# Retention stage of a hybrid decoder block: the norm goes to POOL and ScalarE, gate weights are split earlier, gate banks are single, and ten modulation rows move in

## The chip, the cores and the metric

The kernel runs on one core of a Trainium2 chip. The metric is the device time of one execution in microseconds. Three runs of the kernel before took 2174.5, 2175.4 and 2175.61 us; the median is 2175.4 us.

An engine has a queue of its own and works through it strictly in order, and engines meet through semaphores. The engines are named as in the profile: PE is TensorE (PEld its weight loads), DVE is VectorE, ACT is ScalarE, POOL is GpSimd, SP is SyncE, which here only issues transfers. PSUM has eight banks of 128 x 512 float32 numbers; matmuls write there. SBUF is the memory that all engines read.

## What is computed

A decoder block on 1024 tokens with 1024 channels: a conditioning vector gives six rows of shifts and scales (`w_ada`), a mixer runs retention and dilated attention side by side, and an MLP follows. The part that the change touches is retention: 4 heads, key width 256, value width 512, in 8 chunks of 128 tokens, then a norm over each head's 512 channels, a gain and offset, and a gate:

```
mod = jax.nn.silu(c) @ w_ada[l] + b_ada[l]
...
s = jnp.einsum('bhid,bhjd->bhij', qi, ki) * inner_decay[None]
o = (jnp.einsum('bhij,bhje->bhie', s, vi)
     + jnp.einsum('bhid,bhde->bhie', qi, state) * q_decay[None, :, :, None])
state = (state * chunk_decay[None, :, None, None]
         + jnp.einsum('bhjd,bhje->bhde', ki * k_decay[None, :, :, None], vi))
...
ro = ((ro - mu) * lax.rsqrt(var + GN_EPS)).transpose(0, 2, 1, 3).reshape(B, S, RET_V_W)
ro = (ro * gn_g.astype(jnp.float32) + gn_b.astype(jnp.float32)).astype(h.dtype)
ret_out = (jax.nn.silu(rg) * ro) @ w_ret_out
```

## The kernel before

Every float32 product is made of three matmuls: each operand is split into a high part (a rounded copy, usually by ScalarE) and a low part (the operand less its high part, usually by DVE), and low x high, high x low and high x high are summed in PSUM (`mm3`; lines 207, 209 and 211 are its three matmuls). A weight of 128 x 1024 that comes in as `raw` is split so by `split_w` (lines 197 and 198) into two tiles.

The work is a list of steps, run in the order in which they were added. A step has loads (weights, each with a function that prepares it) and a body. Up to three `raw` tiles of 512 KB are in flight, issued on SP in the order of the list. Within its body a step calls `ahead(room)` at a point of its choosing; there the next step's loads are prepared, that is, split, or, with `mod_load`, multiplied with the conditioning vector into one column of the modulation (a DVE product of 128 x 1024 with an accumulator, then a 128 x 1 addition). At the end of a body each next load takes the place of the prepared one.

In order of time: queries and keys (to about 603 us), values (603 to 712 us), retention (32 chunks, 712 to 980 us), then attention. In the first two stages `mod_turn` is called once a turn, 38 turns in the first and 40 in the values stage. It loads rows of `w_ada` in two buffers that lie in the tile `cossin` and multiplies each with the vector two rows later; `NV` is the number of rows that go this way, and the `while` condition sets their pace. In the values stage `va`, `vb`, `vc` are the products of weights (their low parts `vwl`, line 1328) with the normed input; `v_post` sums them (`vr`), splits them (`vo`) and stores them in HBM (`vd`), from where a chunk later fetches its values.

A chunk (`chunk(h, c)`, g = 8h + c) does, in TensorE's order:

- `kv`, the product of its keys and values for the state (two of 128 x 512), not for the last chunk of a head;
- `RG[h][c] - 1` units of the gate projection (`rg_mm`; a unit is one eighth of a contraction for two banks, six matmuls);
- the scores of the next chunk and the transposes of its keys (`s_kt`: tiles `sT`, `kT`);
- `o`: the state before times the queries (six matmuls) and the scores times the values (three);
- the transposes of the previous chunk's normed output (`on_T`: tile `oT`);
- one more gate unit.

Eight units make one set: one of the head's four gate weights, of which three are computed here and the fourth (`srg` 3) is read back from HBM.

Around that, the other engines of a chunk before: DVE adds the state (line 745), ScalarE copies it rounded (749) and DVE takes the low part (750), half after half. Behind this stands `ahead(2)`, the split of the next chunk's gate weight where one falls due, then the scores: ScalarE copies them out of PSUM (652), DVE adds and multiplies with the decay (653, 654), ScalarE makes the high parts (663, 664), DVE the low ones (666, 668). ScalarE and POOL split the queries and keys of two chunks later (`jit_qk`: tile `j`, lines 616 and 617). At the end comes the norm: DVE takes mean and variance (772, 773), multiplies the variance and adds epsilon (774), POOL raises it to -1/2 (775), DVE multiplies with the decay (776) and centres and scales `o` into `on` (778). Then the gate: when a set has come to its end in this chunk, ScalarE takes silu of both its banks in one instruction (710). In the first four chunks of a head ScalarE scales a quarter of the last head's result (688), DVE multiplies it with the gate (690) and SP stores it (`y`, 691).

PSUM in retention: tag `mm` has two tiles of two banks, tag `s` four of one bank (scores, kT, kv, o, oT). Gate weights are loads of chunks 0, 2 and 5 of each head.

Of the kernel before, what the change touches and what calls it, by code (L numbers as in the profile page):

```python
# [21 lines left out]
H = 4  # L22
# [17 lines left out]
CS_KDEC = 128  # L40
CS_QD = 132
CS_QD2 = 136
CS_ONE = 140
# [97 lines left out]
def block_kernel(ctx, tc, io, stop=None, dbg=None):  # L141
# [3 lines left out]
    def fv(t):  # L145
        return t.bitcast(F32)
# [6 lines left out]

    def banks(single):

        if PS:
            PS["ctx"].close()
        PS["i"] = PS.get("i", 0) + 1
        PS["ctx"] = ExitStack()
        PS["p"] = PS["ctx"].enter_context(tc.tile_pool(name=f"psum{PS['i']}", bufs=2, space=bass.MemoryType.PSUM,  # L160
                                                       reuse_waits="tile"))
        PS["n"] = 8 if single else 4

    banks(True)

    def ps_mm(name):
        return PS["p"].tile([P, 2, 512], F32, tag="mm", bufs=2, name=name)

    def ps_s(name, shape=(P, 512)):
# [342 lines left out]
    def etile(name, dt=F32):  # L512
        return R["p"].tile([P, 1024], dt, tag="E", bufs=12, name=name)

# [89 lines left out]
    def flat(ps):  # L604
        return ps.rearrange("p a b -> p (a b)")
# [23 lines left out]

    def s_kt(i):  # L630

# [33 lines left out]
        if pk is not None:  # L665
            nc.vector.scalar_tensor_tensor(flat(kl), flat(pk), kd, fv(flat(kh)), op0=ALU.mult, op1=ALU.subtract)
            hd["k", g] = (kh, kl)
        nc.vector.tensor_sub(sml, sm, fv(smh))

    def on_T(h, c):  # L670

        po = ps_s(f"oT{h}{c}", (P, 4, P))
        on = hd["o", h, c]
        if c == 0:
            hd["on", h] = [etile(f"on{h}{e}") for e in range(4)]
        for e in range(4):
            nc.tensor.transpose(po[:, e, :], on[:, e * P:(e + 1) * P], ident)
        for e in range(4):
            nc.scalar.copy(hd["on", h][e][:, c * C:(c + 1) * C], po[:, e, :])

    def u_final(h, es=range(4), queue=nc.sync):
        for e in es:
            i = h * 4 + e
            t = hd["on", h][e]
            for hf in range(2):
                neg = 16 if hf == i % 2 else 0
                b = t[:, 512 * hf:512 * hf + 512]
                nc.scalar.activation(b, b, AF.Identity, scale=gnv[0][:, neg + i:neg + i + 1],
                                     bias=gnv[1][:, neg + i:neg + i + 1])
            nc.vector.tensor_mul(t, t, hd["srg", h, e])  # L690
            queue.dma_start(y_d[h][:, 2 * (i % 2):2 * (i % 2) + 2, e // 2], t.rearrange("p (t x) -> p t x", t=2))

    RG = ((6, 2, 2, 3, 3, 3, 3, 2),) + ((3,) * NC,) * (H - 1)

    def rg_mm(n):

        for _ in range(n):
            if hd.get("rgk", NK) == NK:
                hd["rgk"], hd["rgw"], hd["rgp"] = 0, hd["rgws"].pop(0), ps_mm("rg")
            proj_mm(hd["rgp"], hd["rgw"], [hd["rgk"]])  # L700
            hd["rgk"] += 1
            if hd["rgk"] == NK:
                hd["rgs"] = hd["rgp"]

    def rg_out(h, c):

        if "rgs" in hd:
            e = {1: 0, 2: 0, 4: 1, 5: 1, 7: 2}[c]
            hd["srg", h, e] = etile(f"srg{h}{e}")
            nc.scalar.activation(hd["srg", h, e], flat(hd.pop("rgs")), AF.Silu)  # L710
        if c == 6:
            hd["srg", h, 3] = etile(f"srg{h}3")
            nc.sync.dma_start(hd["srg", h, 3], srg_d[h])

    def chunk(h, c, ahead, w=None):
# [19 lines left out]
        if g == 0:  # L735
            s_kt(1)
        rg_mm(1 if g == 0 else RG[h][c] - 1)
        for i, kv in enumerate(kvs):
# [5 lines left out]
            else:  # L744
                nc.vector.scalar_tensor_tensor(st[:, i, :], st[:, i, :], float(GAMMA[h] ** C), kv,  # L745
                                               op0=ALU.mult, op1=ALU.add)
        if g > 0:
            for i in range(len(kvs)):
                nc.scalar.copy(sh1[:, i, :], st[:, i, :])  # L749
                nc.vector.tensor_sub(sl1[:, i, :], st[:, i, :], fv(sh1[:, i, :]))  # L750
        if g == 0:
            jit_qk(2)
        ahead(2)
        if 0 < g < NG - 1:
            s_kt(g + 1)
        po = ps_s(f"o{h}{c}")
# [9 lines left out]
        if g > 0:  # L766
            on_T(*divmod(g - 1, NC))
        rg_mm(0 if g == 0 else 1)
        bn = p.tile([P, 6], F32, tag="bn", bufs=2, name=f"bn{h}{c}")
        ba = p.tile([P, 2], F32, tag="ba", bufs=2, name=f"ba{h}{c}")  # L770
        gr = p.tile([P, 1], F32, tag="gr", bufs=2, name=f"gr{h}{c}")
        nc.vector.bn_stats(bn, po)
        nc.vector.bn_aggr(ba, bn)
        nc.vector.tensor_scalar(gr, ba[:, 1:2], ct[:, CS_QD2 + h:CS_QD2 + h + 1], GN_EPS, op0=ALU.mult, op1=ALU.add)
        nc.gpsimd.tensor_tensor(gr, gr, mhalf[:, 0:1], op=ALU.pow)
        nc.vector.tensor_mul(gr, gr, ct[:, CS_QD + h:CS_QD + h + 1])
        on = p.tile([P, DV], F32, tag="on", bufs=1, name=f"onm{h}{c}")
        nc.vector.tensor_scalar(on, po, ba[:, 0:1], gr, op0=ALU.subtract, op1=ALU.mult)
        hd["o", h, c] = on
        rg_out(h, c)  # L780
        if h > 0 and c < 4:
            u_final(h - 1, (c,))

    def wsplit(ap):
        return ap, split_w
# [453 lines left out]

    NV = 32  # L1240
    turn = {"n": 0, "i": 0}

    def mod_turn():

        turn["n"] += 1
        while turn["i"] < NV + 2 and 7 * turn["n"] > 16 * turn["i"]:
            i = turn["i"]
            turn["i"] += 1
            t = cs[:, i % 2]
            if i > 1:  # L1250
                m = G1 + i - 2
                nc.vector.scalar_tensor_tensor(t, t, 1.0, cb, op0=ALU.mult, op1=ALU.mult, accum_out=mods[:, m:m + 1])
            if i < NV:
                nc.sync.dma_start(t, io["w_ada"][G1 + i])
            if i == NV + 1:
                m = mods[:, G1:G1 + NV]
                nc.vector.tensor_add(m, m, vec[:, VC_BADA + G1:VC_BADA + G1 + NV])
# [126 lines left out]
    def values(ahead):  # L1384
# [42 lines left out]
        R["state"] = R["p"].tile([P, 2, DV], F32, name="state")  # L1427
        banks(False)

    steps.add(first_values, manual=True)  # L1430
    steps.add(more_values, manual=True)
    steps.add(queries_keys, manual=True)

    for h in range(H):
        for c in range(NC):
            steps.add((lambda h, c: lambda ahead, *w: chunk(h, c, ahead, *w))(h, c),
                      ([wsplit(io["w_rg"][3 * h + (0, 2, 5).index(c)])] if c in (0, 2, 5) else []),
                      manual=True)
# [392 lines left out]
    def att_step(pair, a):  # L1831

        def body(*args):
            ps = ps_mm(f"ak{pair}1{a}")
            gen = with_sums(proj_gen(ps, args[-1]))
# [992 lines left out]
def _constants():  # L2828
# [9 lines left out]
    for h in range(H):  # L2838
# [3 lines left out]
        cst[:, CS_KDEC + h] = np.exp(lg * (C - 1 - i)) / 16.0  # L2842
        cst[:, CS_QD + h] = np.exp(lg * (i + 1))
        cst[:, CS_QD2 + h] = np.exp(2 * lg * (i + 1))
    cst[:, CS_ONE] = 1.0
# [71 lines left out]
```

## Time and profile before

| | us |
|---|---|
| median of three runs | 2175.4 |
| the profiled execution, its own time | 2173.28 |
| its span in the profile | 2171.3 |
| mean granted clock of TensorE | 0.999 |

A busy time is the sum of an engine's instructions, without those that only issue or branch. Matmuls overlap (a matmul of 128 x 512 is issued while the previous one drains), so in a listing of single matmuls the distance between starts counts, not the length. In listings "a<-b,c" is an instruction that writes tile a from tiles b and c, and what stands in brackets is the idle time before it with what ended it. Two lines of the page on transfers in retention and before it, median us from issue to landing at the end:

```
cossin<-in_w_ada_dram SPq DMA_DIRECT2D x32, 512.0 KB, 3.5
v<-vd SPq DMA_DIRECT2D x32, 512.0 KB, 4.3
```

### The profile page before, as it was taken

The page shows a single profiled execution, that of the slowest core. Times are in us where ns is not written, and L with a number is a line of the kernel's source. Part 1 is how long each engine was busy: PE and PEld are TensorE (multiplying, and loading weights), DVE is VectorE, ACT ScalarE, POOL GpSimd, SP SyncE. Part 2 cuts the span into 40 slices and gives each one's busy share as a digit, 9 for nine tenths or more (in the row PEclk, how much of TensorE's full clock was granted, in tenths as well). Part 3 has the DMA queues.
Part 4 walks back from the last instruction along what each step waited for, and adds up shares of the span by engine and source line. Part 5 has one row for each costly group of instructions (what it writes and reads, how often), then busy time and mean ns, then how long its engine had stood idle before and what let it go on. Part 6 is the DMA issues. An engine that isn't in the chain of part 4 may idle for free. (4 is left out here: it accounts for less than half of the span.)

```text
span 2171.3 us, 27289 instructions
## 1 busy us (share of the span) xinstructions
PE 2144.7 (99%) x10036; PEld 1782.4 (82%) x10036; DVE 1520.4 (70%) x2358; ACT 959.3 (44%) x1757; POOL 165.7 (8%) x199
## 2 busy tenths in 40 slices
PE   8999999999999999999999999999999999999998
PEld 6888888888887788888888888888778888888887
DVE  6886777777656677776667644677876665877855
ACT  5543322323334455556656625434454455533413
POOL 0001111100001112211110000001000000000003
PEclk9999999999999999999999999999999999999999
DMA  9859998835588744436877366653144435645322
GB/s 383 282 208 309 285 306 265 243 117 194 186 301 303 234 148 151 160 127 197 218 194 196 115 245 211 217 191 132 64 175 160 150 136 193 253 135 173 109 88 78
DMA packets 162674, 425.18 MB, mean 196 GB/s; under 512 B 28005, under 2 KB 55916, under 8 KB 159468
## 3 DMA queue, kind: packets, MB, share of 16 engines
q1 hardware_dynamic: 150264, 374.90, 48.3%
q0 software_dynamic: 9584, 48.24, 9.9%
q8 instruction: 79, 1.29, 0.2%
q10 hardware_dynamic: 2692, 0.30, 0.1%
q14 instruction: 55, 0.45, 0.1%
HBM read 324.13 MB, written 160.32 MB: 223 GB/s over the span
## 5 line engine op out<-in xcount | busy, mean ns | idle before, releaser
L207 PE MATMUL qap<-hh,qaw 128*128 128x512 f32 x264 | 102.7, 389 | 0.0
L209 PE MATMUL qap<-hl,qaw 128*128 128x512 f32 x264 | 102.7, 389 | 0.0
L211 PE MATMUL qap<-hh,qaw 128*128 128x512 f32 x264 | 102.7, 389 | 0.0
L617 POOL TENSOR_TENSOR j<-qk,j 128x512 fp32r<-128x512 f32 x32 | 42.8, 1338 | 454.8 <-ACT j L616 454.8
L2235 POOL TENSOR_TENSOR accnf<-accnf,sqnf 128x256 f32<-128x256 f32 (+1 forms) x18 | 16.6, 922 | 609.6 <-ACT sqnf L2231 609.6
L2339 ACT ACTIVATE a<-a 128x512 f32<-128x512 f32 x48 | 30.3, 631 | 72.8 <-DVE a L2338 71.3
L749 ACT CAST stateh<-state 128x512 fp32r<-128x512 f32 x54 | 32.9, 622 | 57.8 <-DVE state L745 55.7
L209 PEld LDWEIGHTS qap<-hl,qaw 128*128 128x128 f32 x264 | 49.5, 188 | 10.4
L211 PEld LDWEIGHTS qap<-hh,qaw 128*128 128x128 f32 x264 | 49.6, 188 | 10.3
L207 PEld LDWEIGHTS qap<-hh,qaw 128*128 128x128 f32 x264 | 49.5, 188 | 10.2
L2547 ACT CAST w2h<-w2s 128x512 fp32r<-128x512 f32 x36 | 22.4, 621 | 80.3 <-DVE w2s L2585 80.3
L264 DVE TENSOR_TENSOR fw<-w1r,fw 128x512 fp32r<-128x512 f32 x48 | 32.9, 688 | 33.6 <-ACT fw L254 33.6
L264 DVE TENSOR_TENSOR qaw<-wa,qaw 128x512 fp32r<-128x512 f32 x66 | 44.0, 687 | 9.4 <-ACT qaw L254 9.4
L2070 DVE TENSOR_TENSOR rwl<-rwl,rwh 128x1024 fp32r<-128x1024 f32 x25 | 30.2, 1221 | 29.0 <-ACT rwh L2100 29.0
L207 PE MATMUL fp<-h2h,fw 128*128 128x512 f32 x128 | 50.0, 390 | 0.0
L209 PE MATMUL fp<-h2l,fw 128*128 128x512 f32 x128 | 49.8, 389 | 0.0
L211 PE MATMUL fp<-h2h,fw 128*128 128x512 f32 x128 | 49.8, 389 | 0.0
L207 PE MATMUL roa<-rh,rwl 128*128 128x512 f32 x128 | 49.8, 389 | 0.0
L209 PE MATMUL roa<-rl,rwh 128*128 128x512 f32 x128 | 49.8, 389 | 0.0
L211 PE MATMUL roa<-rh,rwh 128*128 128x512 f32 x128 | 49.8, 389 | 0.0
L1603 ACT ACTIVATE P<-P,ng 128x128 f32<-128x128 f32 (+1 forms) x96 | 41.9, 438 | 17.6 <-DVE ng L1595 17.5
L292 DVE TENSOR_TENSOR qat<-qat,qap 128x512 f32<-128x512 f32 x22 | 15.1, 688 | 42.8 <-PE qap L211 35.8
(3089 smaller groups left out, 7187.8 us busy)
## 6 DMA issues: line engine op xcount, KB each, us to landing
cossin<-in_w_ada_dram SPq DMA_DIRECT2D x32, 512.0 KB, 3.5
v<-vd SPq DMA_DIRECT2D x32, 512.0 KB, 4.3
w1r<-in_w_ff_dram SPq DMA_DIRECT2D x32, 512.0 KB, 4.6
yt<-y POOLq DMA_DIRECT2D x24, 512.0 KB, 7.5
xsd<-as SPq DMA_DIRECT2D x24, 512.0 KB, 3.1
w2r<-in_w_ff2s_dram SPq DMA_DIRECT2D x24, 512.0 KB, 6.4
em<-in_w_ada_dram SPq DMA_DIRECT2D x16, 512.0 KB, 10.2
wrvs<-in_w_rv_dram POOLq DMA_DIRECT2D x16, 512.0 KB, 9.8
```

Source lines behind the costliest of these rows:

```text
L207: nc.tensor.matmul(o, wl, xh, start=first, stop=False, skip_group_check=skip)
L209: nc.tensor.matmul(o, wh, xl, start=False, stop=False, skip_group_check=skip)
L211: nc.tensor.matmul(o, wh, xh, start=False, stop=last, skip_group_check=skip)
L264: nc.vector.tensor_sub(t[:, 512:], src, fv(t[:, :512]))
L292: nc.vector.tensor_sub(u, u, b)
L617: nc.gpsimd.tensor_sub(t[:, 1], src, fv(t[:, 0]))
L749: nc.scalar.copy(sh1[:, i, :], st[:, i, :])
L1603: nc.scalar.activation(v, v, AF.Exp, bias=ng[:, blk:blk + 1], accum_out=st[:, g, blk, 2 + a:3 + a])
L2070: nc.vector.tensor_sub(lo, fv(lo), fv(hi))
L2235: (nc.vector if f == 7 else nc.gpsimd).tensor_add(G["acc", key], G["acc", key], sq)
L2339: nc.scalar.activation(o, o, AF.Relu)
L2547: nc.scalar.copy(hi, src)
```

## The change

- **Norm.** The decay is taken into epsilon: with e = eps times gamma^(-2(i+1)), (var + e)^(-1/2) is the whole scale, so the product with the decay goes. DVE adds e to the variance; POOL makes minus the mean, the power, and their product; ScalarE makes `on` from `o` as Identity with a column of scale and a column of bias.
- **PSUM.** In retention tag `rg` has three tiles of one bank, tag `s` five; the old division comes back at the first attention step. A gate set takes two `rg` tiles, and its silu, two instructions of 128 x 512, stands right behind its last unit.
- **Order in a chunk.** ScalarE copies both halves of the state, then DVE takes the first low part; the second stands in `s_kt` ahead of the low part of the scores. `ahead(2)` stands behind `s_kt` in place of ahead of it. The scaling of the last head (ScalarE) stands ahead of `on`; its product (DVE) and its store (SP) wait for the next chunk, behind `ahead` and before `o`'s statistics.
- **Copies of `oT`.** Two copies of 128 x 2 x 128 in place of four of 128 x 128.
- **Gate weights.** The loads are attached where the running count of units first needs them; that is chunks 0, 2, 4 and 7 of head 0, 1, 4 and 7 of heads 1 and 2, 1 and 3 of head 3. The last head's units become 4, 4, 4, 3, 3, 3, 3, 0 in place of 3 each.
- **Modulation rows.** `NV` 22 in place of 32, one row every second turn in place of seven in sixteen. Ten rows become loads of retention's chunks: chunk 6 of head 0, and 4, 5 and 6 of the others, so that their products run in the chunk before each.

```diff
 
-    def banks(single):
+    def banks(single, ret=False):
 
...
                                                        reuse_waits="tile"))
-        PS["n"] = 8 if single else 4
+        PS["n"] = 8 if single else 5 if ret else 4
 
     banks(True)
 
     def ps_mm(name):
         return PS["p"].tile([P, 2, 512], F32, tag="mm", bufs=2, name=name)
+
+    def ps_rg(name):
+        return PS["p"].tile([P, 512], F32, tag="rg", bufs=3, name=name)
 
...
             hd["k", g] = (kh, kl)
+        if mid:
+            mid()
         nc.vector.tensor_sub(sml, sm, fv(smh))
...
                                      bias=gnv[1][:, neg + i:neg + i + 1])
-            nc.vector.tensor_mul(t, t, hd["srg", h, e])
-            queue.dma_start(y_d[h][:, 2 * (i % 2):2 * (i % 2) + 2, e // 2], t.rearrange("p (t x) -> p t x", t=2))
-
-    RG = ((6, 2, 2, 3, 3, 3, 3, 2),) + ((3,) * NC,) * (H - 1)
+
+            def mul(t=t, i=i, e=e):
+                nc.vector.tensor_mul(t, t, hd["srg", h, e])
+                queue.dma_start(y_d[h][:, 2 * (i % 2):2 * (i % 2) + 2, e // 2], t.rearrange("p (t x) -> p t x", t=2))
+
+            if late:
+                return mul
+            mul()
+
+    RG = (6, 2, 2, 3, 3, 3, 3, 2), (3,) * NC, (3,) * NC, (4, 4, 4, 3, 3, 3, 3, 0)
 
     def rg_mm(n):
 
         for _ in range(n):
             if hd.get("rgk", NK) == NK:
-                hd["rgk"], hd["rgw"], hd["rgp"] = 0, hd["rgws"].pop(0), ps_mm("rg")
+                hd["rgk"], hd["rgw"], hd["rgp"] = 0, hd["rgws"].pop(0), [ps_rg(f"rg{i}") for i in range(2)]
             proj_mm(hd["rgp"], hd["rgw"], [hd["rgk"]])
             hd["rgk"] += 1
             if hd["rgk"] == NK:
-                hd["rgs"] = hd["rgp"]
+                i = hd["rgi"] = hd.get("rgi", -1) + 1
+                t = hd["srg", i // 3, i % 3] = etile(f"srg{i // 3}{i % 3}")
+                for j, ps in enumerate(hd["rgp"]):
+                    nc.scalar.activation(t[:, 512 * j:512 * j + 512], ps, AF.Silu)
 
     def rg_out(h, c):
 
-        if "rgs" in hd:
-            e = {1: 0, 2: 0, 4: 1, 5: 1, 7: 2}[c]
-            hd["srg", h, e] = etile(f"srg{h}{e}")
-            nc.scalar.activation(hd["srg", h, e], flat(hd.pop("rgs")), AF.Silu)
         if c == 6:
...
             s_kt(1)
-        rg_mm(1 if g == 0 else RG[h][c] - 1)
+        rg_mm(1 if g == 0 else max(RG[h][c] - 1, 0))
         for i, kv in enumerate(kvs):
...
                                                op0=ALU.mult, op1=ALU.add)
-        if g > 0:
-            for i in range(len(kvs)):
+        def low(i):
+            nc.vector.tensor_sub(sl1[:, i, :], st[:, i, :], fv(sh1[:, i, :]))
+
+        if g > 0 and kvs:
+            for i in range(2):
                 nc.scalar.copy(sh1[:, i, :], st[:, i, :])
-                nc.vector.tensor_sub(sl1[:, i, :], st[:, i, :], fv(sh1[:, i, :]))
+            low(0)
         if g == 0:
             jit_qk(2)
-        ahead(2)
+            ahead(2)
         if 0 < g < NG - 1:
-            s_kt(g + 1)
+            s_kt(g + 1, (lambda: low(1)) if kvs else None)
+        if g > 0:
+            ahead(2)
+        if "um" in hd:
+            hd.pop("um")()
         po = ps_s(f"o{h}{c}")
...
             on_T(*divmod(g - 1, NC))
-        rg_mm(0 if g == 0 else 1)
+        rg_mm(min(RG[h][c], 1) if g > 0 else 0)
         bn = p.tile([P, 6], F32, tag="bn", bufs=2, name=f"bn{h}{c}")
         ba = p.tile([P, 2], F32, tag="ba", bufs=2, name=f"ba{h}{c}")
-        gr = p.tile([P, 1], F32, tag="gr", bufs=2, name=f"gr{h}{c}")
+        gr = p.tile([P, 3], F32, tag="gr", bufs=2, name=f"gr{h}{c}")
         nc.vector.bn_stats(bn, po)
         nc.vector.bn_aggr(ba, bn)
-        nc.vector.tensor_scalar(gr, ba[:, 1:2], ct[:, CS_QD2 + h:CS_QD2 + h + 1], GN_EPS, op0=ALU.mult, op1=ALU.add)
-        nc.gpsimd.tensor_tensor(gr, gr, mhalf[:, 0:1], op=ALU.pow)
-        nc.vector.tensor_mul(gr, gr, ct[:, CS_QD + h:CS_QD + h + 1])
+        nc.vector.tensor_scalar_add(gr[:, 0:1], ba[:, 1:2], ct[:, CS_EQ + h:CS_EQ + h + 1])
+        nc.gpsimd.tensor_tensor(gr[:, 2:3], ba[:, 0:1], ct[:, CS_NEG:CS_NEG + 1], op=ALU.mult)
+        nc.gpsimd.tensor_tensor(gr[:, 1:2], gr[:, 0:1], mhalf[:, 0:1], op=ALU.pow)
+        nc.gpsimd.tensor_tensor(gr[:, 2:3], gr[:, 1:2], gr[:, 2:3], op=ALU.mult)
+        if h > 0 and c < 4:
+            hd["um"] = u_final(h - 1, (c,), late=True)
         on = p.tile([P, DV], F32, tag="on", bufs=1, name=f"onm{h}{c}")
-        nc.vector.tensor_scalar(on, po, ba[:, 0:1], gr, op0=ALU.subtract, op1=ALU.mult)
+        nc.scalar.activation(on, po, AF.Identity, scale=gr[:, 1:2], bias=gr[:, 2:3])
         hd["o", h, c] = on
         rg_out(h, c)
-        if h > 0 and c < 4:
-            u_final(h - 1, (c,))
 
...
 
-    NV = 32
+    NV = 22
     turn = {"n": 0, "i": 0}
 
     def mod_turn():
 
         turn["n"] += 1
-        while turn["i"] < NV + 2 and 7 * turn["n"] > 16 * turn["i"]:
+        while turn["i"] < NV + 2 and turn["n"] > 2 * turn["i"]:
             i = turn["i"]
...
         R["state"] = R["p"].tile([P, 2, DV], F32, name="state")
-        banks(False)
+        banks(False, True)
 
     steps.add(first_values, manual=True)
     steps.add(more_values, manual=True)
     steps.add(queries_keys, manual=True)
 
+    RGW, n = [], 0
+    for g in range(NG):
+        RGW += [g - (g > 2)] * (n < 8 * len(RGW) + 1 <= n + RG[g // NC][g % NC])
+        n += RG[g // NC][g % NC]
+    late_mods = iter(range(G1 + NV, 48))
     for h in range(H):
         for c in range(NC):
             steps.add((lambda h, c: lambda ahead, *w: chunk(h, c, ahead, *w))(h, c),
-                      ([wsplit(io["w_rg"][3 * h + (0, 2, 5).index(c)])] if c in (0, 2, 5) else []),
+                      ([wsplit(io["w_rg"][RGW.index(NC * h + c)])] if NC * h + c in RGW else []) +
+                      ([mod_load(next(late_mods))] if NC * h + c == 6 or h > 0 and c in (4, 5, 6) else []),
                       manual=True)
```

More of the change, by code (lines that the diff above doesn't have):

```diff
@@ L40 @@
 CS_KDEC = 128
-CS_QD = 132
-CS_QD2 = 136
+CS_NEG = 132
+CS_EQ = 136
 CS_ONE = 140
@@ L512, in etile @@
     def etile(name, dt=F32):
-        return R["p"].tile([P, 1024], dt, tag="E", bufs=12, name=name)
+        return R["p"].tile([P, 1024], dt, tag="E", bufs=4, name=name)
     y_d = [dram.tile([P, 4, 2, 512], F32, name=f"y{h}") for h in range(H)]
@@ L628, in chunk_tiles, with s_kt @@
         R["j"] = p.tile([P, 2, 4, C], F32R, tag="j", bufs=2, name="j2")
-    def s_kt(i):
+    def s_kt(i, mid=None):
         p = R["p"]
@@ L674, in on_T, with u_final @@
         if c == 0:
-            hd["on", h] = [etile(f"on{h}{e}") for e in range(4)]
+            hd["on2", h] = [R["p"].tile([P, 2, 1024], F32, tag="EO", bufs=4, name=f"on{h}{e}") for e in range(2)]
+            hd["on", h] = [hd["on2", h][e // 2][:, e % 2] for e in range(4)]
         for e in range(4):
             nc.tensor.transpose(po[:, e, :], on[:, e * P:(e + 1) * P], ident)
-        for e in range(4):
-            nc.scalar.copy(hd["on", h][e][:, c * C:(c + 1) * C], po[:, e, :])
-    def u_final(h, es=range(4), queue=nc.sync):
+        for e in range(2):
+            nc.scalar.copy(hd["on2", h][e][:, :, c * C:(c + 1) * C], po[:, 2 * e:2 * e + 2, :])
+    def u_final(h, es=range(4), queue=nc.sync, late=False):
         for e in es:
@@ L1833, in body @@
         def body(*args):
+            if pair == a == 0:
+                banks(False)
             ps = ps_mm(f"ak{pair}1{a}")
@@ L2842, in _constants @@
         cst[:, CS_KDEC + h] = np.exp(lg * (C - 1 - i)) / 16.0
-        cst[:, CS_QD + h] = np.exp(lg * (i + 1))
-        cst[:, CS_QD2 + h] = np.exp(2 * lg * (i + 1))
+        cst[:, CS_NEG] = -1.0
+        cst[:, CS_EQ + h] = GN_EPS * np.exp(-2 * lg * (i + 1))
     cst[:, CS_ONE] = 1.0
```

## The prediction

> **What bounds the kernel now.** I read the page's busy shares first, to see which engine has no room.
>
> ```profile
> span 2171.3 us, 27289 instructions
> PE 2144.7 (99%) x10036; PEld 1782.4 (82%) x10036; DVE 1520.4 (70%) x2358; ACT 959.3 (44%) x1757; POOL 165.7 (8%) x199
> ```
>
> TensorE is busy for 2144.7 of 2171.3 us, so all its pauses together are about 26.6 us. The change takes no matmul away; it can gain only such pauses, and it loses by every new one. So I next looked at where the pauses lie, in the busy time of each engine in stretches around the change: last half of the queries/keys stage with the first values, values, retention's start, retention, attention's start. The columns are the stretch, its length, then PE, PEld, DVE, ACT and POOL busy with instruction counts, granted clock, DMA share, GB/s.
>
> ```profile
> 640.00:712.00 72.00, 69.38 (x304) 56.45 (x302) 46.30 (x65) 28.20 (x42) 8.33 (x10) 1.00 0.87 329
> 712.00:750.00 38.00, 36.21 (x174) 29.18 (x175) 24.07 (x55) 17.10 (x44) 6.95 (x8) 1.00 0.71 232
> 750.00:980.00 230.00, 229.85 (x1140) 191.62 (x1140) 173.39 (x362) 123.58 (x307) 47.56 (x54) 1.00 0.44 146
> ```
>
> In the 230 us that hold nearly all 32 chunks TensorE is idle for 0.15 us, at a granted clock of 1.00. The pauses of this region are 2.6 us in the values stage and 1.8 at retention's start. Third view: what TensorE waited for between 590 and 1000 us (sum, times, longest).
>
> ```profile
> PE vc L209 <- DVE vwl L1328: 1.9, 2, 1.5
> PE rg L207 <- DVE vr L1367: 1.1, 1, 1.1
> PE kv L207 <- ACT state L763: 0.9, 1, 0.9
> ...
> PE o L207 <- DVE state L745: 0.2, 1, 0.2
> ```
>
> These few microseconds are the whole stock of gain. Fourth, one chunk, since what matters is how late each engine may be before TensorE notices (start, length, engine, line).
>
> ```profile
> 859.65 0.28 PE L638 MATMUL sT<-j 128*128 128x256 f32 x1
> ...
> 868.29 0.28 PE L638 MATMUL sT<-j 128*128 128x256 f32 x1
> 868.42 1.28 DVE L745 SCALAR_TENSOR_TENSOR state<-state,kv 128x512 f32<-128x512 f32 x2
> 869.13 1.22 ACT L749 CAST stateh<-state 128x512 fp32r<-128x512 f32 x2 [2.67 <-DVE state L745]
> 869.15 0.49 PE L207 MATMUL o<-stateh,j 128*128 128x512 f32 x1
> 870.26 0.26 ACT L652 COPY sm<-sT 128x128 f32<-128x128 f32 x1
> 872.18 0.69 DVE L772 BATCH_NORM_STATS2 bn<-o 128x6 f32<-128x512 f32 x1
> 873.12 0.21 DVE L774 TENSOR_SCALAR gr<-ba,ct 128x1 f32<-128x1 f32 x1
> 873.17 0.39 PE L207 MATMUL kv<-v,kl 128*128 128x512 f32 x1
> 873.78 0.54 POOL L775 TENSOR_TENSOR gr<-gr,ct 128x1 f32<-128x1 f32 x1
> 874.53 0.62 PE L207 MATMUL rg<-hh,raw_6386l 128*128 128x512 f32 x2
> 875.89 0.62 PE L207 MATMUL rg<-hh,raw_6386l 128*128 128x512 f32 x2
> ```
>
> A chunk lasts 868.29 - 859.65 = 8.64 us. With o's first matmul as zero, kv starts at 4.02, the two gate units behind it at 5.38 and 6.74 (1.36 each, six matmuls), the copy of the state at 0.0 and the statistics (bn) at 3.03.
>
> **The change part by part: gains.** *Values stage.* The rows' loads and products were at seven rows to 16 turns and lasted almost through this stage; now one per two turns, and only 22 rather than 32.
>
> ```profile
> cossin<-in_w_ada_dram SPq DMA_DIRECT2D x17, 512.0 KB, 3.5
> vd<-vo SPq DMA_DIRECT2D x16, 512.0 KB, 10.1
> 649.41 0.60 ACT L1362 ACTIVATE vo<-va 128x512 fp32r<-128x512 f32 x1 [4.44 <-DMA vd<-vo]
> L1252 DVE SCALAR_TENSOR_TENSOR cossin<-cossin,cb x32: 1212/1219/1309, 510.5 to 706.2; 128x1024 f32<-128x1024 f32 x32
> ```
>
> Of the 17 loads of 512 KB issued from 590 us on, about 12 leave, and about 13 products of 1.22 us, 16 us of DVE. The vwl pauses of 1.9 us come where ScalarE waited 4.44 us for a store that took 10.1 us to land on busy queues, and then delivered late. I take these 1.9 as gone, with about 0.6 of smaller ones: -2.5 (bounds 0 and -3.5, all pauses named). The wait for vr, the last value add before retention, hangs on the values themselves and stays.
>
> *Retention's start.* The 0.9 for state L763 goes, since the split of the next gate weight and ScalarE's copies no longer stand ahead of it, and the three or four o-waits of 0.2 to 0.3 at each head's second chunk go with the copies made first: -1.7, of which I give back 0.3 for the first chunk's new waits. Bounds -2 and +1.
>
> *Moved work that costs nothing by itself.* DVE loses the centring (0.81 us a chunk), one small product and its wait for POOL:
>
> ```profile
> L778 DVE TENSOR_SCALAR onm<-o,ba,gr 128x512 f32<-128x512 f32 x32 | 25.9, 810 | 3.4
> L776 DVE TENSOR_TENSOR gr<-gr,ct 128x1 f32<-128x1 f32 x32 | 5.1, 160 | 28.2 <-POOL gr L775 28.2
> L775 POOL TENSOR_TENSOR gr<-gr,ct 128x1 f32<-128x1 f32 x32 | 17.5, 546 | 15.2 <-DVE gr L774 15.2
> L688 ACT ACTIVATE on<-on,gnt 128x512 f32<-128x512 f32 x32 | 24.3, 833 | 0.0
> L710 ACT ACTIVATE srg<-rg 128x1024 f32<-128x1024 f32 x12 | 12.6, 1050 | 3.1 <-PE rg L211 3.1
> L690 DVE TENSOR_TENSOR on<-on,srg 128x1024 f32<-128x1024 f32 x16 | 19.5, 1220 | 5.6 <-ACT on L688 5.4
> ```
>
> Per chunk that is 0.81 + 0.16 + 28.2/32 = 1.85 us less on DVE; POOL gets two more operations of 0.55 (bounds 0.16, as on DVE, and 0.6) and ScalarE one Identity with a column for scale and bias, 0.83 by the form nearest to it. No engine becomes full by this: DVE was at 173 of 230 us, ScalarE at 124, POOL at 48. That cover hides them as averages only. ScalarE runs its queue in order, and behind the centring (`on`) now stand, in turn, the gate's silu, both state copies, the scores' copy and with it DVE's next chain.
>
> **The costs.** *A gate set ends inside a pair of units.* The gate's PSUM goes from two double banks to three single ones. A set is eight units for two banks; the next set's second bank is the old set's first, so its matmul waits for that half's silu. Where units 16 and 17 of a head are the two behind kv, no other TensorE work lies between: chunk 5 of heads 1 and 2, chunk 4 of head 3. The first unit starts at 5.38, its bank is closed at about 6.75, and TensorE wants the bank back at 6.74 + 0.23 = 6.97. The silu comes behind the previous chunk's `on`. How late is that? In that chunk DVE has, ahead of the statistics, the modulation row (product 1.22, and its small adds, 1.4) and the deferred product of the last head (1.22). By the rows:
>
> - DVE's state adds end at 0.55; ScalarE's copies 0.0 to 1.22, the scores' copy 0.26 behind them: 1.5.
> - DVE: the two score operations, kl, the second low part, the last low part of the scores. In the timeline of before the one from the scores' copy (870.26) to bn (872.18) took 1.9; with the 0.69 of a low part moved in between and less waiting I take 2.1: 3.6.
> - Row 1.4, product 1.22: 6.2. Statistics to gr ready, 873.12 + 0.21 - 872.18 = 1.15: 7.35. POOL begins 0.45 later (873.78) and does power and product in 1.1: 8.9. `on` with its hand-over 0.9: 9.8. Half a silu, 0.53, and hand-over: 10.45.
>
> The wait is 10.45 - 6.97 = 3.5 us at each. Besides, the loop from `on` to `on` must fit into 8.64 us, or it carries lateness on. It is 9.8 by the steps above, 8.4 without the row, and 11.0 where a weight split (DVE 1.22) comes too, which is one chunk ahead of these. So the copies start up to 11.0 - 8.64 = 2.4 us late; part of it is met by a shorter second wait, kl (ready at about 2.7, wanted at 4.02) shows another 1. I take +1.5, so 5.0 at each of heads 1 and 2; in head 3, whose first three chunks have four units and last 1.36 longer, 2.5. Together 12.5. From below: with the lateness of the bank alone where no row and no product stood ahead (bn at 3.03 rather than 6.2, `on` at 6.6, the bank at 7.3 plus hand-over and a small queue) it would be at least 0.5 each, and I hold 1.9 for the lower bound with one of the two products ahead: 5.7.
>
> *POOL beside DVE.* POOL's subtraction for j now falls beside DVE's low parts, split, row or product, not beside the statistics.
>
> ```profile
> L617 POOL TENSOR_TENSOR j<-qk,j 128x512 fp32r<-128x512 f32 x30 | 38.8, 1292 | 203.7 <-ACT j L616 203.7
> 696.33 1.72 DVE L1328 TENSOR_TENSOR vwl<-vwl,vwh 128x1024 fp32r<-128x1024 f32 x1
> 1453.32 1.29 POOL L2235 TENSOR_TENSOR accn<-accn,sqn 128x512 f32<-128x512 f32 x1 [274.78 <-ACT sqn L2231]
> 1454.15 1.54 DVE L198 TENSOR_TENSOR raw_12456l<-raw,raw_12456h 128x1024 fp32r<-128x1024 f32 x1 [1.63 <-ACT raw_12456h L197]
> ```
>
> Beside a POOL pass these DVE passes took 1.54 and 1.72 against 1.22 alone: 0.3 to 0.5 more. With 0.5 in each of the chunks 1 to 4 that run up to a boundary I add 1.9 per boundary, 5.7: the boundaries cost 18.2. Bounds 0 and the whole 1.29 per chunk (about 4.6 per boundary, 13.8, total 26.3).
>
> [...] The rows above do not bear a full exclusion out, for each pass was lengthened by less than half of the other's 1.29.
>
> *Into attention.* The last head's units are moved ahead, chunk 7 has none, and the first attention weight's split now stands behind `on` of chunk 6 in ScalarE's queue.
>
> ```profile
> 973.59 1.08 ACT L197 CAST raw_7655h<-raw 128x1024 fp32r<-128x1024 f32 x1
> 975.34 1.21 DVE L198 TENSOR_TENSOR raw_7655l<-raw,raw_7655h 128x1024 fp32r<-128x1024 f32 x1
> 980.75 0.62 PE L207 MATMUL ak<-hh,raw_7655l 128*128 128x512 f32 x2
> ```
>
> Before, it was ready at 976.55, 4.2 us ahead of its use. After, TensorE reaches it 1.36 us sooner, and the high part follows `on` (some 4 us later than 973.6), then 1.08 + 1.21: about 1.7 late. Bounds 0 and 3.5.
>
> *Queues.* Ten rows of 512 KB and the stores of the last head come on SP's queue in retention. Stores wait for a later product with the fetches of q, k and v behind them, but those are issued three chunks (26 us) ahead and land in about 5, and the DMA share there is 0.44. Nothing; if the cover were gone, a late j would show as a TensorE wait on POOL.
>
> **Sum.** -2.5 - 1.4 + 12.5 + 5.7 + 1.7 = +16.0; some of these pauses will cover one another (a late bank lets DVE catch up), for which I take 0.6 off: +15.4. The profiled run of before took 2173.28 us, 2.0 more than its span, and lies 2.1 below the median. So the span goes from 2171.3 to 2186.7, that run to 2188.7, and the median from 2175.4 to 2190.8.
>
> **The rivals.**
> - *The boundaries are covered* (the other side). DVE has 1.85 us less per chunk, and if ScalarE's `on` of the boundary's previous chunk ends before about 6.4 after o's start, the silu is in time and only the gains are left: -3.9, with the 0.9 to 1 us of small waits that a freer DVE may end besides -4.5: 2171. For it: the averages, DVE 173 and now some 160 of 230 with the moved rows. Against: the order on DVE, where statistics stand behind 2.6 us of row and product.
> - *Each boundary costs only its own wait*, the loop carries nothing and POOL and DVE pass each other: 5.7 to 10.5 with -3.9 and +1 to +1.7: +3 to +8, 2178 to 2183, say 2180.
> - *POOL and DVE exclude each other.* Then 26.3 - 3.9 + 1.7 = +24: 2199.5. For it, that both rows show some lengthening; against, that it is less than half of 1.29. [...]
> - *The loads were not the cause* of the values stage's pauses: everything else as forecast, 2193, inside the main range.
>
> **How the numbers follow.** Main case 0.42, own range 2185 to 2196. Boundaries covered 0.20. Own waits only 0.20. Exclusion 0.18. A measurement here tells about 0.2%, 4.35 us, from no change: below 2171.05 is faster, above 2179.75 slower. The covered case lies on that edge: 0.09 faster, 0.11 same; of the own-waits case 0.08 is same. So faster 0.09, same 0.19, slower 0.72. The range goes from 2171, which takes in most of the covered case, to 2200, which takes in the exclusion.
>
> **What would show it.** In the profile after: vwl gone from the list of TensorE's waits and the stretch 640 to 712 with less than 1 us of idle time; a wait of rg on ScalarE's silu (`srg`), 3 to 7 us each, three times, in chunks 5, 5 and 4 of heads 1 to 3; `on` waiting for POOL, and DVE's row and product ahead of the statistics; one wait of ak on the weight split. Wrong: retention's stretch still without idle time (then the loop fits), or a wait of o, kv or the scores on j or on the state that exceeds those of rg (then the bound is another than the gate's banks).

## The result, and the profile after

The changed kernel takes 2188.07 us (median of six runs, 2186.63 to 2191.11) against 2174.95 us before (six runs): 13.1 us more, a ratio of 1.0062 with a 95% interval of 1.0049 to 1.0075. The profiled execution is the slowest of the six, 2191.11 us, so its span is 17.9 us longer than the one of before; about 2.1 of these lie outside the change's region (the first value product starts 1.0 us later, and from attention's first matmul to the end 1.1 are added), about 15.8 in it.

The head of the page of after, then its stretches (columns as before: length, PE, PEld, DVE, ACT and POOL busy, granted clock, DMA share, GB/s):

```profile
span 2189.2 us, 27312 instructions
...
PE 2151.1 (98%) x10036; PEld 1788.7 (82%) x10036; DVE 1505.1 (69%) x2304; ACT 976.5 (45%) x1737; POOL 187.5 (9%) x263
```

```profile
640.00:712.00 72.00, 71.22 (x315) 58.67 (x314) 35.83 (x43) 29.13 (x44) 7.13 (x10) 1.00 0.78 278
712.00:750.00 38.00, 38.00 (x192) 31.87 (x191) 23.42 (x51) 20.47 (x45) 9.87 (x16) 1.00 0.61 205
750.00:990.00 240.00, 227.07 (x1092) 188.51 (x1092) 164.73 (x322) 132.02 (x278) 66.66 (x104) 0.96 0.48 156
```

The values stage's idle time fell from 2.6 to 0.8 us, the start's from 1.8 to nothing; retention, which had none, now has 12.9 us, and its granted clock has fallen to 0.96. No engine became full: DVE has less to do than before. What TensorE waits for between 590 and 1010 us (sum, times, longest):

```profile
PE rg L210 <- ACT srg L718: 11.0, 3, 4.0
PE o L210 <- DVE state L756: 2.0, 2, 1.0
PE ak L210 <- DVE raw_8071l L201: 1.3, 1, 1.3
PE rg L210 <- DVE vr L1386: 0.8, 1, 0.8
```

vwl and the state's copy are gone from the list; the gate's bank stands in their place, three times. The first of them, in TensorE's chunk 5 of head 1 while the other engines are still at the norm of chunk 4, in the timeline (start, length, engine, line; in brackets the idle time before):

```profile
816.29 0.49 PE L210 MATMUL o<-stateh,j 128*128 128x512 f32 x1 [0.99 <-DVE state L756]
...
820.12 1.41 POOL L620 TENSOR_TENSOR j<-qk,j 128x512 fp32r<-128x512 f32 x1 [3.59 <-ACT j L619]
820.30 2.31 DVE L467 SCALAR_TENSOR_TENSOR raw<-raw,cb 128x1024 f32<-128x1024 f32 x1
...
822.73 1.22 DVE L698 TENSOR_TENSOR on<-on,srg 128x1024 f32<-128x1024 f32 x1
823.03 0.39 PE L210 MATMUL rg<-hh,raw_6050l 128*128 128x512 f32 x1
823.86 0.69 DVE L790 BATCH_NORM_STATS2 bn<-o 128x6 f32<-128x512 f32 x1
...
825.24 0.54 POOL L794 TENSOR_TENSOR gr<-gr,ct 128x1 f32<-128x1 f32 x1
825.86 0.19 POOL L795 TENSOR_TENSOR gr<-gr 128x1 f32<-128x1 f32 x1
826.08 0.78 ACT L799 ACTIVATE onm<-o,gr 128x512 f32<-128x512 f32 x1 [5.50 <-POOL gr L795]
826.76 1.07 ACT L718 ACTIVATE srg<-rg 128x512 f32<-128x512 f32 x2
827.40 0.80 PE L210 MATMUL rg<-hh,raw_6050l 128*128 128x512 f32 x1 [3.98 <-ACT srg L718]
828.00 1.05 PE L212 MATMUL rg<-hl,raw_6050h 128*128 128x512 f32 x2
```

Read it backwards from 827.40: TensorE waits for the silu, the silu for `on`, `on` (after 5.50 us of idle ScalarE) for POOL, POOL for the statistics, and these for the row's product, 2.31 us, and the last head's product. The last line shows one thing more: two matmuls span 1.05 us there, where two spanned 0.62 before. The granted clock, which stands behind the five busy times in each row, tells why:

```profile
820.00:823.00 3.00, 3.00 (x15) 2.47 (x14) 2.96 (x6) 0.58 (x3) 1.41 (x1) 1.00 0.07 29
...
825.75:827.40 1.65, 0.00 (x0) 0.00 (x1) 0.60 (x2) 1.32 (x3) 0.22 (x2) 0.50 0.98 274
...
829.00:830.00 1.00, 1.00 (x5) 0.81 (x4) 0.07 (x1) 0.00 (x0) 0.00 (x0) 0.50 0.72 283
...
833.00:834.00 1.00, 1.00 (x7) 0.83 (x6) 1.00 (x2) 0.62 (x1) 0.11 (x1) 1.00 0.00 0
```

After the wait of 4.0 us TensorE works at half speed for some 5 us, until 832.4. The clock had fallen within the wait already, at 825.6, 2.2 us after the last matmul ended.

### The profile page after: what moved, and what is told of

Same layout as the page of the kernel before. It is cut to its first block, busy times and chain, and to the rows that moved or that the text cites. A ratio compares the mean times of both kernels' runs of the same rounds, so it can differ in the third digit from the quotient of the medians.

```text
span 2189.2 us, 27312 instructions
## 1 busy us (share of the span) xinstructions
PE 2151.1 (98%) x10036; PEld 1788.7 (82%) x10036; DVE 1505.1 (69%) x2304; ACT 976.5 (45%) x1737; POOL 187.5 (9%) x263
## 3 DMA queue, kind: packets, MB, share of 16 engines
q8 instruction: 79, 1.29, 0.2%
## 5 line engine op out<-in xcount | busy, mean ns | idle before, releaser
L620 POOL TENSOR_TENSOR j<-qk,j 128x512 fp32r<-128x512 f32 x32 | 52.4, 1638 | 406.3 <-ACT j L619 406.3
L759 DVE TENSOR_TENSOR statel<-state,stateh 128x512 fp32r<-128x512 f32 x54 | 37.0, 686 | 30.7 <-ACT stateh L763 30.7
L210 PEld LDWEIGHTS qap<-hh,qaw 128*128 128x128 f32 x264 | 49.6, 188 | 10.2
L799 ACT ACTIVATE onm<-o,gr 128x512 f32<-128x512 f32 x32 | 24.9, 779 | 68.8 <-POOL gr L795 68.8
## 6 DMA issues: line engine op xcount, KB each, us to landing
em<-in_w_ada_dram SPq DMA_DIRECT2D x16, 512.0 KB, 10.2
```

The lines of the kernel that those rows point to most:

```text
L210: nc.tensor.matmul(o, wl, xh, start=first, stop=False, skip_group_check=skip)
L620: nc.gpsimd.tensor_sub(t[:, 1], src, fv(t[:, 0]))
L799: nc.scalar.activation(on, po, AF.Identity, scale=gr[:, 1:2], bias=gr[:, 2:3])
```

## The experiments

Each kernel differs from the changed kernel by the diff shown (one starts from the kernel before). Times are medians; "before" is the same kernel before, run beside them on the same chip, 2173.7 to 2174.5. Three theories: *chain* (the silu is late since it stands behind `on`, and `on` behind the row and the product on DVE), *bank* (three banks are too few, or the set ends at the wrong place, whatever stands ahead), and for POOL beside DVE *exclusion* against *sharing*.

**Rows in other chunks.**

```diff
-([mod_load(next(late_mods))] if NC * h + c == 6 or h > 0 and c in (4, 5, 6) else []),
+([mod_load(next(late_mods))] if NC * h + c in (6, 7, 14, 15, 16, 22, 23, 24, 30, 31) else []),
```

> The ten modulation rows of retention run in chunks 5, 6 and 7 instead of 3, 4 and 5; all else as in the changed kernel. Chain theory (the silu stands behind `on`, `on` behind POOL, POOL behind the statistics, the statistics behind row and product): without the row, which took 2.3 us in chunks 3 and 4, the gate's wait falls from 4.0 to at most 1.5 us at heads 1 and 2 and from 3.0 to about 1, the wait of o for the state (1.0 twice) goes, and the granted clock stays at 1.00 after each; about 12 us less, 2174 to 2178. Bank theory (three banks are too few whatever stands ahead): gate waits above 3 us stay, time 2185 to 2189.

Measured: 2179.51 us, ratio to before 1.0024 (1.0015 to 1.0033), some 8.6 less than the changed kernel. Waits of TensorE, and two stretches behind the first and the second gate wait:

```profile
PE rg L210 <- ACT srg L718: 6.8, 3, 2.6
...
PE oT L683 <- ACT onm L799: 0.9, 1, 0.9
```

```profile
825.00:830.00 5.00, 5.00 (x19) 4.20 (x20) 3.21 (x7) 2.45 (x7) 0.00 (x0) 0.66 0.26 97
895.50:900.50 5.00, 4.99 (x27) 4.21 (x28) 3.40 (x7) 3.40 (x9) 0.77 (x1) 1.00 0.27 102
```

The time lies in neither theory's range. The row is worth what the chain says in direction, and o's wait for the state went, but the gate's waits stopped at 2.6, not at 1.5: the expectation was too low by the last head's product, which still stands there. And the clock: behind one wait of 2.6 us it fell, behind the next of the same length it did not.

**The last head's product behind the statistics.**

```diff
-        if "um" in hd:
-            hd.pop("um")()
         po = ps_s(f"o{h}{c}")
...
         nc.gpsimd.tensor_tensor(gr[:, 2:3], gr[:, 1:2], gr[:, 2:3], op=ALU.mult)
+        if "um" in hd:
+            hd.pop("um")()
         if h > 0 and c < 4:
```

> The deferred product of the last head stands behind the statistics rather than ahead of them; all else as in the changed kernel. Chain theory: the statistics come 1.2 us sooner in chunks 1 to 4, so each gate wait shrinks by 1.2 to 2 us (to about 2 to 2.8 at heads 1 and 2, 1 to 1.8 at head 3), and the half-clock stretch goes where the wait falls below what the 1.6 us wait of the kernel before showed; 2176 to 2184. Bank theory: no change, 2188.

Measured: 2182.48 us, 1.0033 (1.0021 to 1.0045).

```profile
PE rg L210 <- ACT srg L718: 7.1, 3, 2.7
PE o L210 <- ACT onm L799: 2.0, 2, 1.0
```

As the chain theory has it: the gate's waits fell from 11.0 to 7.1, by 1.3 each.

**Both together.** The two diffs above in one kernel.

> Rows in chunks 5 to 7 and the deferred product behind the statistics, together. Each alone left gate waits of about 2.6 us (heads 1, 2) and 1.8 (head 3). Chain theory: together nothing but the scores' operations and the weight split stands ahead of the statistics, so the waits shrink again by 1.2 to 2: 0.6 to 1.4 and 0.4 to 0.8; time 2174 to 2177. If 2.6 us is a floor of the three banks and of ScalarE's order (POOL's three steps, `on`, silu), the waits stay at 2 us or more and the time at 2179.

Measured: 2173.57 us, 0.9992 (0.9983 to 1.0002).

```profile
PE ak L210 <- DVE raw_7980l L201: 1.5, 1, 1.5
PE oT L683 <- ACT onm L799: 0.9, 1, 0.9
PE rg L210 <- DVE vr L1386: 0.8, 1, 0.8
PE rg L210 <- ACT srg L718: 0.7, 3, 0.2
```

The gate's three waits are 0.2 each, with three banks and the set ending where the change ends it: so the bank theory falls as the cause, and 0.2 is its own share. The chain is the cause, and both works ahead of the statistics are needed for it to be as long as it was. The time is that of the kernel before, no better: ak still waits 1.5 us for its weight, and behind that wait the profile has 3.4 us at the half clock.

**Four banks.**

```diff
-        return PS["p"].tile([P, 512], F32, tag="rg", bufs=3, name=name)
+        return PS["p"].tile([P, 512], F32, tag="rg", bufs=4, name=name)
...
-        PS["n"] = 8 if single else 5 if ret else 4
+        PS["n"] = 8 if single else 4
```

> Tag rg with four banks and tag s with four, all else as in the changed kernel. Chain and bank theory both expect the gate's waits on the silu to go, with the half-clock stretches after them: 18 us less, against at most 3 us of new waits of the other tag; 2170 to 2174, and below the kernel before by the values stage's and the start's gain. If the lateness of `on` itself is what costs (whatever the banks), a wait of oT on `on` or of o on the state takes its place: 2180 or more.

Measured: 2180.55 us, 1.003 (1.0018 to 1.0043).

```profile
PE o L210 <- ACT onm L799: 5.6, 8, 1.0
PE kT L648 <- DVE state L756: 2.9, 3, 1.1
```

The gate's waits are gone and half of the loss is still there: `on` reads o's bank, and with one `s` bank less the next o waits until `on` has read it, as kT does for the state's sum. The lateness finds the next tile. This was the case named last in the expectation.

**Set ends away from the next set.**

```diff
-    RG = (6, 2, 2, 3, 3, 3, 3, 2), (3,) * NC, (3,) * NC, (4, 4, 4, 3, 3, 3, 3, 0)
+    RG = (6, 2, 2, 3, 3, 3, 3, 2), (3, 3, 3, 3, 2, 3, 3, 4), (3, 3, 3, 3, 2, 3, 3, 4), (4, 4, 4, 2, 3, 3, 3, 1)
```

> Only the units per chunk are changed: 3,3,3,3,2,3,3,4 in heads 1 and 2 and 4,4,4,2,3,3,3,1 in head 3, so that a gate set ends behind kv with scores, o and oT between it and the next set, and one unit is left for the last chunk. Bank theory (in the form that the four banks left open: only the place of the set's end costs): gate waits gone, 2171 to 2173. Chain theory: the gate's waits go, but `on` is as late as before, so 1 to 3 us a head of o's waits on `on` or on the state come in their place, as with four banks: 2177 to 2182. The wait of ak on the weight split, 1.3, falls to 0.5 or less by the last chunk's unit.

Measured: 2180.2 us, 1.0027 (1.0016 to 1.0038).

```profile
PE o L210 <- DVE state L756: 6.5, 4, 2.4
PE ak L210 <- ACT srg L718: 0.9, 1, 0.9
```

Again the gate's waits are gone and another takes their place: o's for the state, DVE's sum of which stands behind the statistics. In the last chunk, ak no longer waits for its weight but 0.9 for a silu, an expectation that missed.

**`on` back on DVE.**

```diff
-        nc.scalar.activation(on, po, AF.Identity, scale=gr[:, 1:2], bias=gr[:, 2:3])
+        nc.vector.tensor_scalar(on, po, gr[:, 1:2], gr[:, 2:3], op0=ALU.mult, op1=ALU.add)
```

> The centring `on` is put back on DVE, with POOL's scale and bias; all else as in the changed kernel. Chain theory: `on` no longer stands ahead of the silu and the state's copies in ScalarE's queue, so the gate's wait is at most 0.6 us and the state's copies start on time; in exchange DVE waits about 0.8 us a chunk for POOL and works 0.8 more: 2170 to 2177. If the silu is late for another reason (banks, or ScalarE itself), the waits stay near 3 to 4 us: 2186 or more.

Measured: 2183.66 us, 1.0041 (1.0026 to 1.0056); the forecast of 2170 to 2177 was wrong.

```profile
PE o L210 <- DVE onm L799: 9.0, 7, 2.7
...
PE rg L210 <- ACT srg L718: 0.7, 3, 0.2
```

The gate's wait is indeed gone from 11.0 to 0.7, so ScalarE's queue is the link between `on` and the silu. But now o waits 9.0 us, in seven places, for `on` itself, which DVE can only begin behind the row, the product, the statistics and POOL's steps (818.33 us where o waited until 819.20).

**POOL beside DVE.** Only j's low part of chunks 3 and 4 of heads 1 to 3 goes to DVE.

```diff
-        nc.gpsimd.tensor_sub(t[:, 1], src, fv(t[:, 0]))
+        (nc.vector if i > 8 and i % 8 in (5, 6) else nc.gpsimd).tensor_sub(t[:, 1], src, fv(t[:, 0]))
```

> Of the changed kernel, only the low part of j that is made in chunks 3 and 4 of heads 1 to 3 goes to DVE (0.69 by the forms of 128 x 512), so that no POOL pass runs beside the row's product there. Exclusion theory (a DVE pass that meets a POOL pass waits for its whole rest): the row's product takes 1.22 rather than 2.31 us in these chunks, DVE gains 1.1 less 0.7 a chunk, and each gate wait shrinks by 0.4 to 1 us; 2182 to 2187. Sharing theory (both slowed a little, the row's product long for another reason such as its transfer): 2.3 us stays, the waits grow by 0.7 or more: 2188 to 2192.

Measured: 2185.19 us, 1.0046 (1.0029 to 1.0063). The first boundary's row, and TensorE's waits:

```profile
820.07 1.22 DVE L467 SCALAR_TENSOR_TENSOR raw<-raw,cb 128x1024 f32<-128x1024 f32 x1
```

```profile
PE rg L210 <- ACT srg L718: 10.0, 3, 3.9
...
PE o L210 <- DVE state L756: 1.0, 2, 0.5
```

The time is as the exclusion theory has it; the first two gate waits shrank by less than its 0.4 us (the longest from 4.0 to 3.9). The row's product takes 1.22 us without a POOL pass beside it, 2.31 with one: exclusion. In the profile of after POOL's pass ran from 820.12 to 821.53, and the row, issued at 820.30, ended 1.08 behind it. The last head's product in chunk 2 was held up in the same way (from 801.21 for 2.32 us, POOL's pass from 801.03 to 802.45). In the other order it is POOL's pass that is lengthened, here to 2.19 us from the 1.29 that it takes alone; in chunk 1 of head 1 there:

```profile
791.30 1.22 DVE L698 TENSOR_TENSOR on<-on,srg 128x1024 f32<-128x1024 f32 x1
791.49 2.19 POOL L620 TENSOR_TENSOR j<-qk,j 128x512 fp32r<-128x512 f32 x1 [3.95 <-ACT j L619]
```

In these three pairs the pass that started first took 1.41, 1.42 and 1.22 us, at most 0.13 above its usual time, and the one that started within it was lengthened, by 1.09, 1.10 and 0.90.

**The rows alone**, on the kernel before: `NV = 22`, the pace of one row in two turns, and the ten loads in retention as in the change; norm, banks and order untouched.

```diff
-    NV = 32
+    NV = 22
...
-        while turn["i"] < NV + 2 and 7 * turn["n"] > 16 * turn["i"]:
+        while turn["i"] < NV + 2 and turn["n"] > 2 * turn["i"]:
...
+                      ([mod_load(next(late_mods))] if NC * h + c == 6 or h > 0 and c in (4, 5, 6) else []),
```

> The kernel before with the slower pace of rows and the ten rows in retention alone, norm, banks and order as before. If the slower pace is what ended the values stage's waits for vwl (1.9 us): these go, 712 is reached 2.5 to 3 us sooner; the row's product stands ahead of the scores there and may cost up to 1 us in each of three heads: 2172 to 2175. If the values stage's gain came from another part: vwl's waits stay, 2175 to 2178.

Measured: 2176.84 us, 1.0011 (1.0002 to 1.0021).

```profile
PE kv L207 <- DVE kl L666: 4.8, 4, 1.5
PE rg L207 <- DVE vr L1367: 0.8, 1, 0.8
```

No wait for vwl is left; retention's first matmul of the gate starts at 708.69 against 712.43. But the same rows cost 4.8 us in retention, more than the 3 expected, and the time missed its range of 2172 to 2175: in that order they stand ahead of the scores' operations and so of kl.

**All mended.** Rows out of chunks 3 and 4, product behind the statistics, and the split set ends, together (the three diffs above).

> All three: rows in chunks 5 to 7, deferred product behind the statistics, set ends split from the next set, one unit in the last chunk. Chain theory: with neither lateness nor a bank to wait for, what is left is the gain of the values stage and of retention's start, 4 to 6 us below the kernel before: 2169 to 2171. If a shorter chunk (two units, 7.3 us) can't hold the loop, 1 to 2 us of waits a head remain: 2173 to 2176.

Measured: 2170.54 us, 0.9983 (0.9974 to 0.9993). Then with the second of head 0's rows one chunk later:

```diff
-([mod_load(next(late_mods))] if NC * h + c in (6, 7, 14, 15, 16, 22, 23, 24, 30, 31) else []),
+([mod_load(next(late_mods))] if NC * h + c in (6, 8, 14, 15, 16, 22, 23, 24, 30, 31) else []),
```

> As the kernel with rows in chunks 5 to 7, product behind the statistics and set ends split, but the second row of head 0 runs a chunk later, beside no weight split. The wait of oT on `on` at 775 (0.9 us) goes if the row's product behind a split and a POOL pass made it: 2169 to 2170.5. If the first heads' `on` is late for the weight split alone, it stays: 2170.5.

Measured: 2169.74 us, 0.9979 (0.9969 to 0.999). Waits of TensorE between 590 and 1010 us:

```profile
PE ak L210 <- ACT srg L718: 0.9, 1, 0.9
PE rg L210 <- DVE vr L1386: 0.8, 1, 0.8
PE sc L212 <- DVE kl L1569: 0.2, 1, 0.2
```

The wait of oT on `on` is gone as the expectation had it, but against the kernel before, beside which each was run, this kernel is 4.0 us faster and the one ahead of it 3.9: the later row is worth nothing that these runs can tell. Both lie about 18 us below the changed kernel. Last, the same kernel with `on` back on DVE (the diff shown above):

> The same with `on` back on DVE (POOL still makes scale and bias). If the norm on ScalarE is worth something by itself once nothing stands ahead of the statistics: waits of o or oT on DVE's `on` and on the state come up, 1 us a head, 2173 to 2176. If the gain is that of the rows, the order of the state's copies and the start alone: 2169 to 2171.5, no worse than with ScalarE.

Measured: 2173.13 us, 0.9993 (0.9984 to 1.0003), 3.4 us more than with ScalarE.

```profile
PE o L210 <- DVE onm L799: 1.7, 4, 0.6
PE ak L210 <- ACT srg L718: 0.9, 1, 0.9
PE oT L683 <- DVE onm L799: 0.9, 1, 0.9
```

So `on` on ScalarE is a gain once neither the rows nor the last head's product hold up the statistics, and is part of the mended kernel's. POOL makes scale and bias in both, so what these steps are worth on POOL is not shown.

## Why the prediction was right, point by point

Forecast +15.4 us, measured +13.1 in the medians, about 15.8 in the profiled region. The direction, the places and the mechanism held; two terms of the sum were mis-sized and one was missing. That the sum came so near is in part luck.

- *TensorE is full, so only new waits count.* Right; in the kernels here the time followed TensorE's waits and its clock.
- *Values stage, -2.5.* Right: retention's first gate matmul starts 2.8 us sooner relative to the first value product (598.60 to 712.43 before, 599.59 to 710.60 after). The rows alone do it: with them alone it is 4.0 us (598.86 to 708.69).
- *Retention's start, -1.4.* Mis-sized: the first head's chunk 7 is reached another 2.7 us sooner (4.5 in all, less the 1.8 that it stood ahead at the first matmul).
- *Three set ends, 12.5.* The waits were 11.0 for the gate and 2.0 for o, 13.0 in place of 12.5. The steps: `on` was forecast 9.8 us after o's start plus up to 2.4 carried in; it ended at 826.86, 10.6 after o, which had itself waited 1.0. Two of POOL's three steps took 0.19, near the lower bound of 0.16, not 0.55; the row took 1.1 more than forecast. Each of the two works ahead of the statistics was needed, as the two single edits and their sum show.
- *POOL beside DVE, 5.7.* The failed step of the working. I took 0.3 to 0.5 of lengthening as a share of the whole POOL pass; in the two pairs here it was the rest of that pass at the time when DVE's started, less 0.14 us. The weight split at 1454.15 met a POOL pass that had 0.46 left and was lengthened by 0.32; the row's product at 820.30 met one that had 1.23 left and was lengthened by 1.09. The exclusion that I weighed and set aside fits both. Ahead of each of the first two boundaries three DVE passes were lengthened by 1.1 (the last head's product in chunk 2, the row's in 3 and 4), ahead of the third two. Taking POOL's pass away in chunks 3 and 4 was worth about 2.9 us in all, with 10.2 in place of 17.1 us at the half clock in the profiles; 0.7 us of DVE's time was put in its place, so this is not the whole price of exclusion, which no run here shows.
- *The half clock.* Missing from the sum. Measured from o's product with the values in the chunk ahead of each set end to the same product one chunk on, the three boundaries took 6.6, 7.0 and 4.7 us longer than before; the pauses themselves, start to start and less a matmul's usual 0.227, were 4.2, 4.1 and 3.2. The rest, about 2.4, 2.9 and 1.5, together some 6.9 us, are matmuls at a clock of 0.50. It filled the place of the 5.7 by chance; the sum was nearer than its terms.
- *Into attention, +1.7.* Measured 1.3, at the place that was forecast. The prediction's own numbers give 1.2 rather than 1.7: 976.55 + 4.0 for the weight against 980.75 - 1.36 for its use.
- *Queues, nothing.* Right: no wait on a transfer in retention.
- *Rivals.* The loop did not fit. Nor did each boundary cost its own wait alone: lateness was carried on (o's waits of 1.0), and POOL and DVE did hold each other up. Exclusion is real, but its time, 2199.5, was too long: it put the whole 1.29 into four chunks ahead of each boundary, where two or three DVE passes were lengthened by 1.1.

What stays open: why the profiled execution lies 3 us above the median. The half clock came behind one wait of 2.6 us and not behind the next, which could vary the time, but the other executions have no trace here, and their mean granted clocks (0.994 to 0.996, against 0.995 in the profiled one) do not order the times.

## What to carry to other kernels

Where TensorE is full, as here, what moving work to an idle engine is worth was decided by what stands ahead of it in the queues, not by the engine's busy share: follow the chain from the last reader back through each in-order queue, and put the work that nobody waits for behind the statistics that everybody waits for. More buffers did not mend the late producer here; four banks and another place of the set's end each took off about half of the loss and moved the rest of the wait to the next tile. And a wait on TensorE can cost more than its length: in the profile of after the three of 3.0 to 4.0 us each had matmuls at a clock of 0.50 behind them, some 6.9 us in all, and waits of 1.5 and of 2.6 us had them in one case and not in another.

## What the runs showed of the hardware that was not expected

A pause of TensorE of 4.0 us was followed by some 5 us at a granted clock of 0.50, in which matmuls start about 0.43 us apart in place of 0.227; the clock of 1.00 came back at 832.4, while TensorE worked on. In the profile of after all three pauses of 3.0 us and more between values and attention (4.0, 4.0 and 3.0) had a half-clock stretch behind them: 0.51, 0.50 and 0.54 over the next 5.0, 5.5 and 3.3 us. With the rows in other chunks this happened behind one pause of 2.6 us and not behind another (0.66 and 1.00 over the next 5 us). Even a pause of 1.5 us had one, in the kernel with the two works moved:

```profile
979.07 0.81 PE L210 MATMUL ak<-hh,raw_7980l 128*128 128x512 f32 x2 [1.53 <-DVE raw_7980l L201]
```

```profile
979.50:983.00 3.50, 3.50 (x10) 2.75 (x9) 0.62 (x4) 1.71 (x2) 0.93 (x3) 0.51 0.44 150
```

A pause of 1.5 us in the kernel before, up to 658.15, had none (1.00 over 656 to 661), and with the rows alone, where four pauses of up to 1.5 us add up to 4.8, the mean granted clock of the profiled execution is 0.999, as before. The half-clock stretches lasted 3.4 us (979.6 to 983.0 here, 968.9 to 972.3 in the changed kernel) or 6.8 (825.6 to 832.4 in the changed kernel, where the first 1.8 lie within the pause, and 900.7 to 907.5). The clock fell 2.2, 3.2 and 2.8 us after the last matmul ahead of the changed kernel's three pauses ended. What decides whether it falls, and for how long, stays open: no run here changes the length of a pause alone.
